# Hybrid encoder layer: eviction tiles and PSUM banks of the values' stage, early row scales, x first, a denser first attention

## The chip, the cores and the metric

One core of one Trainium2 chip runs the whole kernel. The metric is the device time of one execution in microseconds. The kernel before took 2954.69 us (median of 3 runs, 2953.99 to 2956.52).

## The reference, cut to what matters

One encoder layer is applied to two batches with the same weights: s (1024 tokens, two chunks of 512) and p (512 tokens, one chunk). The width is 2048, so there are 16 slices k of 128 features.

```
h  = rms_norm(x, norm_g) @ w_in      # split into qa ka va ga | qb kb vb gb
oa = window_gqa(qa, ka, va, sink, rel_bias)    # 16 heads, 4 key heads, +/-128 tokens
ob = diff_attention(qb, kb, vb, lam, ...)      # 8 heads, two softmax maps, RMSNorm per head
y  = rms_norm(x + concat(silu(ga) * oa, silu(gb) * ob) @ w_out, final_g)
```

Everything is float32. The kernel reaches that precision with three products of rounded numbers: each operand is split into a rounded part (hi, wh) and the remainder (lo, wl), and hi·wh + lo·wh + hi·wl is summed in PSUM.

## The kernel before, in words

**Stages.** The values' stage of batch s comes first (`in_v_all`, L357). It runs over five groups g of 256 value columns. For each group (`in_v`, L327) eight parts of the weights are used, two slices k each, and each part is 48 matmuls of 256 columns: 2 slices, 2 chunks, 4 token tiles, 3 products (L337, L339, L341). The sums of one group fill four PSUM banks, one bank for two token tiles of one chunk. At the end of a group eight evictions follow: ACT scales and rounds (L351), DVE makes the remainder (L352), both into one tile `ov`, and GpSimd's queue sends it to DRAM (L354). The pool `ev` has two tiles `ov`.

During group 0 the function `before` (L749) also loads x, splits it (L222, L223) and sums its squares. At the end of group 0 it makes the row scales by token (`rstd_cols`, L185, by products with a column of ones). During groups 1 to 4 it takes one step of `bias_rows` (L117) per part: constants, five small products of the bias tables (L130) with a copy to `o` (L132), and loads that spread the rows over 128 partitions. After group 4 `rstd_rows` (L194, called at L771) spreads the row scales over all partitions: four products per chunk with the identity, and a copy by DVE.

Then the feature stage of batch s follows (`in_fm`, L299; `project`, L281). It has 42 tiles of 128 features, each 16 slices times 6 matmuls of 512 columns. Its evictions (L310 to L324) use the tiles `o` and, under the name `sq`, `th`. Other places use the name `sq` too: the squares of `sum_squares` (L179) and those of `normalise` in the second attention (L617).

**Order of the work.** `drive` (L713) weaves a main generator (the projections) and a side one (attention). Each step of the projection reports its cost, and each step of attention is charged a fixed gap, so a smaller gap packs attention steps closer. While the features of s are projected, the first attention of s runs beside it with `GAP_AS` = 2.1. After it, in the same side generator, x of batch p is loaded, squared, summed and scaled (L778 to L788). In the second half the projections of p and all output projections run beside the second attention of s and both attentions of p; there the values' stage of p comes first, with one chunk and four evictions a group.

The source order is not the final order. The framework gives each instruction a place on its engine, by the order of the source and by when its inputs are ready. On each engine the instructions then run in order. A tile pool hands out one set of buffers for each name, and a new tile waits until the last user of its buffer is done. PSUM has eight banks. The pool `psv` of the values' stage has eight buffers under one name, `pp`. The next pool `psp1` takes over the four lower banks, and the attention's pools take the four upper ones.

**Queues.** SP issues nearly all loads, weights among them (`Weights.load`, L248, three tiles ahead). GpSimd's queue issues the stores.

**The lines that matter here.** L207 loads an x tile, L252 a weight tile, L260 and L262 split the weights. L328 takes the banks of a group, L348 the eviction tile:

```
ps = [[psp.tile([P, 2, 256], F32, name="pp") for _ in range(2)] for _ in chs]
...
o = ev.tile([P, 2, 256], F32, name="ov", bufs=2)
```

Of the kernel before, what the change touches and what calls it, by code (L numbers as in the profile page):

```python
# [9 lines left out]
F32 = mybir.dt.float32  # L10
# [20 lines left out]
LB = 2048  # L31
LA = 512
LATE = 4
GAP_AS = 2.1
GAP_BS = 1.05
GAP_AP = 1.7
GAP_BP = 1.3
# [7 lines left out]
def kernel(  # L45
# [71 lines left out]
    def bias_rows(psp, pool):  # L117
        constants()
        yield
        rb = const.tile([33, 24], F32, name="rb")  # L120
        nc.gpsimd.memset(rb[32:33], MASKED)
        dma(out=rb[0:32], in_=rel_bias)
        row_a = dram.tile([16, LA], F32, name="row_a")
        row_b = dram.tile([HB, LB], F32, name="row_b")
        for n in range(1 + LB // TC):
            oh = pool.tile([P, TC], F32, name="xr")
            dma(out=oh[0:33], in_=oh_a if n == 0 else oh_b[:, (n - 1) * TC:n * TC])
            m, heads = (16, rb[:, 0:16]) if n == 0 else (HB, rb[:, 16:24])
            ps = psp.tile([P, 512], F32, name="pp")
            T.matmul(ps[0:m, :], lhsT=heads, rhs=oh[0:33], start=True, stop=True)  # L130
            o = ev.tile([P, TC], F32, name="o", bufs=2)
            V.tensor_copy(o[0:m], ps[0:m, :])  # L132
            dma(out=row_a if n == 0 else row_b[:, (n - 1) * TC:n * TC], in_=o[0:m])
            yield
        for h in range(16):
            dma(out=rep_a[h], in_=row_a[h:h + 1, :].to_broadcast([P, LA]))
            yield
        for h in range(HB):
            dma(out=rep_b[h], in_=row_b[h:h + 1, :].to_broadcast([P, LB]))
            yield  # L140
# [41 lines left out]
        S.activation(out=dst, in_=src, func=AF.Sqrt, scale=1.0 / n, bias=eps)  # L182
        V.reciprocal(out=dst, in_=dst)

    def rstd_cols(acc, psp):  # L185

        ps = psp.tile([P, 512], F32, name="pp")
        for t in range(TC // P):
            T.matmul(ps[:, t:t + 1], lhsT=acc[:, t * P:(t + 1) * P], rhs=ones[:, 0:1], start=True, stop=True)
        rc = nrm.tile([P, TC // P], F32, name="rc", bufs=3)  # L190
        rsqrt_mean(rc, ps[:, 0:TC // P], DM)
        return rc

    def rstd_rows(rc, psp, pool=None, **kw):  # L194

        ps = psp.tile([P, 512], F32, name="pp")
        for t in range(TC // P):
            T.matmul(ps[:, t * P:(t + 1) * P], lhsT=rc[:, t:t + 1].to_broadcast([P, P]), rhs=ident, start=True, stop=True)
        if pool is None:
            return ps  # L200
        rb = pool.tile([P, TC], F32, name="rb", **kw)
        V.tensor_copy(rb, ps)
        return rb
# [37 lines left out]
    class Weights:  # L241


        def __init__(self, wp, order, loads, splits):
            self.wp, self.todo, self.loads, self.splits = wp, order, loads, splits
            self.raw, self.ready = [], []

        def load(self):  # L248
            while self.todo and len(self.raw) < self.loads:
                wr = self.wp.tile([P, 512], F32, name="wr", bufs=self.loads)  # L250
                src = self.todo.pop(0)
                dma(out=wr.rearrange("p (a c) -> p a c", a=src.shape[1]), in_=src)  # L252
                self.raw.append(wr)

        def split(self, n):
# [43 lines left out]
    def in_fm(b, chs, c, psp, wp):  # L299
        ps = yield from project(chs, psp, wp)  # L300
        gate = c >= C_GA
        f = 0.125 if c < C_KB or C_QA <= c < C_KA else 1.0
        for n, ch in enumerate(chs):
            sl = slice(n * TC, (n + 1) * TC)
            o = ev.tile([P, TC], F32, name="o", bufs=2)
            th = ev.tile([P, TC], F32, name="sq", bufs=2)
            hi = th.bitcast(F32R)
            h = ps[n]
            if not b.normed:
                V.scalar_tensor_tensor(out=o, in0=h, scalar=f, in1=b.rb[n], op0=ALU.mult, op1=ALU.mult)  # L310
                h = o
            if gate:
                S.activation(out=th, in_=h, func=AF.Tanh, scale=0.5)
                V.scalar_tensor_tensor(out=o, in0=th, scalar=1.0, in1=h, op0=ALU.add, op1=ALU.mult)
                pdma(out=b.fm[c][:, sl], in_=o)
                continue
            if b.normed:
                S.activation(out=hi, in_=h, func=AF.Copy, scale=f)
                V.scalar_tensor_tensor(out=o, in0=h, scalar=f, in1=th, op0=ALU.mult, op1=ALU.subtract)
            else:  # L320
                S.copy(out=hi, in_=o)
                V.tensor_tensor(out=o, in0=o, in1=th, op=ALU.subtract)
            pdma(out=b.fm[c][:, sl], in_=th)
            pdma(out=b.fml[c][:, sl], in_=o)  # L324
        done.add((b.nm, "fm", c))

    def in_v(b, chs, g, psp, wp, before=None):  # L327
        ps = [[psp.tile([P, 2, 256], F32, name="pp") for _ in range(2)] for _ in chs]  # L328
        for part in range(8):
            wh, wl = wp.next(2, before and (lambda: before(g, part)))  # L330
            for j in range(2):
                k = 2 * part + j
                for n, ch in enumerate(chs):
                    for t in range(4):
                        o = ps[n][t // 2][:, t % 2, :]
                        tok = slice(t * P, (t + 1) * P)
                        T.matmul(o, lhsT=ch.hi[k][:, tok], rhs=wh[:, j, :], start=(k == 0 and t % 2 == 0), stop=False,  # L337
                                 skip_group_check=True)
                        T.matmul(o, lhsT=ch.hi[k][:, tok], rhs=wl[:, j, :], start=False, stop=False,  # L339
                                 skip_group_check=True)  # L340
                        T.matmul(o, lhsT=ch.lo[k][:, tok], rhs=wh[:, j, :], start=False, stop=(k == KT - 1),  # L341
                                 skip_group_check=True)
                yield len(chs) * 12 * 0.109
        if before:
            before(g, 8)
        for n, ch in enumerate(chs):
            for t in range(4):
                o = ev.tile([P, 2, 256], F32, name="ov", bufs=2)  # L348
                f = 1.0 if b.normed else b.rc[n][:, t:t + 1]
                h = ps[n][t // 2][:, t % 2, :]  # L350
                S.activation(out=o[:, 0, :].bitcast(F32R), in_=h, func=AF.Copy, scale=f)  # L351
                V.scalar_tensor_tensor(out=o[:, 1, :], in0=h, scalar=f, in1=o[:, 0, :], op0=ALU.mult, op1=ALU.subtract)  # L352
                tok = slice(n * TC + t * P, n * TC + (t + 1) * P)
                pdma(out=b.v[g][tok], in_=o)  # L354
        done.add((b.nm, "v", g))

    def in_v_all(b, chs, psp, wp, before=None):  # L357
        for g in range(5):
            yield from in_v(b, chs, g, psp, wp, before)

    order_fm = []
    for pr in range(2):
# [372 lines left out]
    def run(g):  # L735
        for _ in g:
            pass
# [1 line left out]
    w_pool = lambda name, bufs: tc.tile_pool(name=name, bufs=bufs, reuse_waits="tile")  # L739

    with tc.tile_pool(name="act2", bufs=KT, side="right", reuse_waits="tile") as act2, w_pool("wp1", 2) as wp1:
        wp = Weights(wp1, tiles_v() + tiles_p(w_fm, order_fm), 3, 2)
        with tc.tile_pool(name="xraw1", bufs=9, side="right", reuse_waits="tile") as xraw, ps_pool("psv", 8, "left") as psp:
            chs = [new_chunk(), new_chunk()]
            accs = [xraw.tile([P, TC], F32, name="acc", bufs=2) for _ in chs]
            bias = bias_rows(psp, xraw)
            squares = []

            def before(g, part):  # L749
                if g > 0:  # L750
                    next(bias, None)
                    return
                late = squares[:] if part == 8 else squares[:-LATE]
                del squares[:len(late)]
                for n, sq in late:
                    V.tensor_tensor(out=accs[n], in0=accs[n], in1=sq, op=ALU.add)
                if part == 8:
                    bs.rc = [rstd_cols(acc, psp) for acc in accs]
                    return
                for k in (2 * part, 2 * part + 1):  # L760
                    for n in range(2):
                        xr = fetch(bs, n, k, xraw)
                        split_x(chs[n], xr, k, (act, act2)[n], ng[:, k:k + 1])
                        if k == 0:
                            sum_squares(accs[n], xr, True)
                        else:
                            squares.append((n, square(xr, xraw)))

            run(in_v_all(bs, chs, psp, wp, before))
            run(bias)  # L770
            bs.rb = [rstd_rows(rc, psp, nrm, bufs=2) for rc in bs.rc]  # L771

        with ps_pool("psp1", 4, "left") as psp, ExitStack() as held:
            raws = []
# [20 lines left out]
    with w_pool("wp2", 3) as wp2, ps_pool("psp2", 2, "left") as psp:  # L795
        wp = Weights(wp2, tiles_v() + tiles_p(w_fm, order_fm) + 3 * tiles_p(w_o, range(KT)), 3, 3)

        def main():
            yield from in_v_all(bp_, [ch_p], psp, wp)
            yield from in_fm_all(bp_, [ch_p], psp, wp)  # L800
            yield from need(("s", "a"), ("s", "b"))
            with tc.tile_pool(name="yp", bufs=1, reuse_waits="tile") as yp:
# [96 lines left out]
```

## Time and profile before

| | |
|---|---|
| median of 3 runs | 2954.69 us |
| the profiled execution | 2958.31 us |
| its span | 2956.5 us |
| mean granted clock of TensorE | 0.986 of 2.4 GHz |
| PE busy | 2884.3 us |
| DVE busy | 1601.6 us |
| ACT busy | 1142.4 us |

The span is the time from the first to the last instruction that the profile holds. The profiled execution's own time is 1.8 us longer than its span and 3.6 us longer than the median of the runs. Busy time of PE counts a matmul until its modelled end, so neighbouring matmuls overlap; the distance between two starts is the time that one takes from the next.

### The profile page before, as it was taken

Reading aid. Unit: us, or ns where it says so; the run is one execution under the profiler, and the core shown is the slowest. Engines: PE = TensorE matmul, PEld = TensorE weight load, DVE = VectorE, ACT = ScalarE, POOL = GpSimd, SP = SyncE. Lnnn points to the kernel's source line nnn. Section 1 sums busy time; section 2 is a strip of 40 time slices with the busy share of each in tenths; the row PEclk is TensorE's granted clock in tenths of the full one; section 3 lists DMA queues with packets and bytes.
Section 4 is the critical chain, followed back from the end, with each engine's and each line's share of the span. In section 5 each row is a group of like instructions: output and inputs, shape, how many; then the busy total and the mean of one; then the engine's idle time right before and its main releaser. Section 6 shows DMA issues by size and latency. Waiting matters only on the chain.

```text
span 2956.5 us, 42517 instructions
## 1 busy us (share of the span) xinstructions
PE 2884.3 (98%) x15370; PEld 2447.1 (83%) x15370; DVE 1601.6 (54%) x3328; ACT 1142.4 (39%) x2329; POOL 307.8 (10%) x554
## 2 busy tenths in 40 slices
PE   8998999999999999998999999999999999999997
PEld 8897888888888887888998888888887888788885
DVE  7122224555555555335666656666477766865633
ACT  6121113333333333124444444444355544543321
POOL 0010001111111111000010000000011100100101
PEclk9999999999999999999999999999999999999998
DMA  6732323342433433226454544443376557853633
GB/s 193 266 106 80 113 76 101 112 135 87 133 118 108 136 108 135 82 89 192 146 156 133 152 142 140 154 129 116 114 213 201 154 165 207 256 157 119 218 121 117
DMA packets 298686, 419.74 MB, mean 142 GB/s; under 512 B 49431, under 2 KB 164119, under 8 KB 297452
## 3 DMA queue, kind: packets, MB, share of 16 engines
q1 hardware_dynamic: 265452, 322.62, 36.4%
q0 software_dynamic: 33024, 94.41, 8.7%
q8 instruction: 121, 1.98, 0.3%
q14 instruction: 89, 0.73, 0.1%
HBM read 322.41 MB, written 107.05 MB: 145 GB/s over the span
## 4 chain that ended last, share of the span: by engine, by line
PE 75%; issue 18%; DMA 3%; DVE 1%; POOL 1%; ACT 1%; SPq 0%; POOLq 0%; DVEq 0%; ACTq 0%
PE pp L291 18%; PE pp L290 18%; PE pp L293 18%; PE s L566 4%; PE s L446 2%; PE tp L588 2%; PE tp L468 2%; PE pp L337 1%; PE pp L341 1%; PE pp L339 1%; PE o_ps L603 1%; PE o_ps L604 1%; PE o_ps L602 1%; PE o_ps L482 1%; PE o_ps L481 1%
## 5 line engine op out<-in xcount | busy, mean ns | idle before, releaser
L290 PE MATMUL pp<-hi,wh 128*128 128x512 f32 x2784 | 1124.9, 404 | 9.9 <-DVE ov L352 9.8
L291 PE MATMUL pp<-lo,wh 128*128 128x512 f32 x2784 | 1107.5, 398 | 0.8 <-DVE lo L236 0.8
L293 PE MATMUL pp<-hi,wl 128*128 128x512 f32 x2784 | 993.0, 396 | 0.6 <-DVE wl L262 0.6
L260 ACT CAST wh<-wr 128x512 fp32r<-128x512 f32 x608 | 375.9, 619 | 954.9 <-PE pp L291 672.8
L262 DVE TENSOR_TENSOR wl<-wr,wh 128x512 fp32r<-128x512 f32 x608 | 418.0, 688 | 558.8 <-ACT wh L260 525.4
L293 PEld LDWEIGHTS pp<-hi,wl 128*128 128x128 f32 x2784 | 525.7, 189 | 121.4 <-DVE wl L262 1.0
L290 PEld LDWEIGHTS pp<-hi,wh 128*128 128x128 f32 x2784 | 526.2, 189 | 106.6 <-DVE ov L352 10.0
L291 PEld LDWEIGHTS pp<-lo,wh 128*128 128x128 f32 x2784 | 526.9, 189 | 96.3 <-DVE lo L236 2.3
L337 PE MATMUL pp<-wh,hi 128*128 128x256 f32 x960 | 276.7, 289 | 19.8 <-ACT hi L222 8.6
L339 PE MATMUL pp<-wl,hi 128*128 128x256 f32 x960 | 272.9, 284 | 1.1 <-DVE wl L262 1.1
L341 PE MATMUL pp<-wh,lo 128*128 128x256 f32 x960 | 273.5, 285 | 0.0
L568 DVE CUSTOM_DVE_ANT_0 t<-s,strip 128x1024 f32<-128x1024 f32 (+1 forms) x192 | 199.5, 1042 | 84.1 <-PE s L566 83.8
L573 ACT ACTIVATE t<-t,nm 128x1024 f32<-128x1024 f32 (+1 forms) x192 | 193.6, 1008 | 125.7 <-DVE nm L568 124.1
L337 PEld LDWEIGHTS pp<-wh,hi 128*128 128x128 f32 x960 | 184.8, 193 | 27.1 <-ACT wh L260 9.4
L339 PEld LDWEIGHTS pp<-wl,hi 128*128 128x128 f32 x960 | 186.1, 194 | 2.6 <-DVE wl L262 1.8
L341 PEld LDWEIGHTS pp<-wh,lo 128*128 128x128 f32 x960 | 184.2, 192 | 0.1
L566 PE MATMUL s<-kk,qq 128*128 128x512 f32 x640 | 181.1, 396 | 1.9 <-DVE nm L568 1.8
L451 ACT ACTIVATE t<-t,nm 128x384 f32<-128x384 f32 (+1 forms) x192 | 110.0, 574 | 167.4 <-DVE nm L447 167.3
L591 DVE TENSOR_TENSOR pl<-tp,ph 128x512 fp32r<-128x512 f32 x160 | 110.1, 688 | 94.5 <-ACT ph L590 93.8
L471 DVE TENSOR_TENSOR pl<-tp,ph 128x512 fp32r<-128x512 f32 (+1 forms) x160 | 93.0, 582 | 107.5 <-ACT ph L470 106.9
L470 ACT CAST ph<-tp 128x512 fp32r<-128x512 f32 (+1 forms) x160 | 79.9, 500 | 181.5 <-PE tp L468 179.8
L447 DVE CUSTOM_DVE_ANT_0 t<-s,bias,nsink 128x384 f32<-128x384 f32 (+1 forms) x192 | 102.4, 570 | 73.2 <-PE s L446 73.2
(117 smaller groups left out, 2976.5 us busy)
## 6 DMA issues: line engine op xcount, KB each, us to landing
wr<-in_w_fm_dram SPq DMA_DIRECT2D x336, 256.0 KB, 3.2
wr<-in_w_o_dram SPq DMA_DIRECT2D x192, 256.0 KB, 3.5
wr<-in_w_v_dram SPq DMA_DIRECT2D x80, 256.0 KB, 3.5
xr<-in_xt_s_dram SPq DMA_DIRECT2D x64, 256.0 KB, 3.5
fm_s<-sq POOLq DMA_DIRECT2D x52, 256.0 KB, 3.6
fml_s<-o POOLq DMA_DIRECT2D x52, 256.0 KB, 3.8
out_dram<-y POOLq DMA_DIRECT2D x48, 256.0 KB, 3.9
v_s<-ov POOLq DMA_DIRECT2D x40, 256.0 KB, 2.5
```

What stands on the lines that cost most here:

```text
L260: S.copy(out=wh, in_=wr)
L262: V.tensor_tensor(out=wl, in0=wr, in1=raw(wh), op=ALU.subtract)
L290: T.matmul(ps[n], lhsT=wh[:, j, :], rhs=ch.hi[k], start=(k == 0), stop=False)
L291: T.matmul(ps[n], lhsT=wh[:, j, :], rhs=ch.lo[k], start=False, stop=False)
L293: T.matmul(ps[n], lhsT=wl[:, j, :], rhs=ch.hi[k], start=False, stop=(k == KT - 1))
L337: T.matmul(o, lhsT=ch.hi[k][:, tok], rhs=wh[:, j, :], start=(k == 0 and t % 2 == 0), stop=False, skip_group_check=True)
L339: T.matmul(o, lhsT=ch.hi[k][:, tok], rhs=wl[:, j, :], start=False, stop=False, skip_group_check=True)
L341: T.matmul(o, lhsT=ch.lo[k][:, tok], rhs=wh[:, j, :], start=False, stop=(k == KT - 1), skip_group_check=True)
L566: T.matmul(s[:, sl], lhsT=u.q[:, m, x, tok], rhs=u.head.kk[:, m, sl], start=(x == 0), stop=(x == 1))
L568: V.tensor_tensor_reduce(out=t, in0=s, in1=u.head.strip[:, x0:x0 + n], scale=-1.0, scalar=3.0e38, op0=ALU.add, op1=ALU.min, accum_out=u.nm ...
L573: S.activation(out=t, in_=t, func=AF.Exp, scale=-1.0, bias=u.nm[:, m:m + 1], accum_out=z1 if m else z0)
L591: V.tensor_tensor(out=pl[:, :, qi, :], in0=tp, in1=raw(ph)[:, :, qi, :], op=ALU.subtract)
```

## The change

- **Eviction tiles.** `in_v` gets a function `out(t)` for its tile. In the values' stage of s the tiles of t = 0 and 2 come from four buffers `ov` in the x pool, those of t = 1 from the two buffers `o`, those of t = 3 from the two buffers `th`. In the stage of p they alternate between `o` and `th`. The tile `th` of the feature stage gets this name of its own instead of `sq`, and the pool `ev` has no `ov` any more.
- **Banks.** The eight banks of the stage of s are two names of four, `p0` and `p1`. Even groups take `p0`, odd ones `p1`. The bias tables' and the row scales' products use `p0`, the column scales and the first identity products `p1`.
- **Row scales early.** `rstd_rows` is called in part 7 of group 1 instead of after group 4.
- **x first.** The first two x tiles are fetched before the first weights, and the first three weight tiles are issued from ACT's queue instead of SP's. Twenty products of the identity with itself stand ahead of everything on PE.
- **Buffers of the x pool.** x and squares have 8 buffers each instead of 9.
- **Denser first attention.** `GAP_AS` is 1.9 instead of 2.1.

```diff
-GAP_AS = 2.1
+GAP_AS = 1.9
@@ bias_rows
-            ps = psp.tile([P, 512], F32, name="pp")
+            ps = psp.tile([P, 512], F32, name="p0", bufs=4)
@@ rstd_cols, and rstd_rows in the same way
-        ps = psp.tile([P, 512], F32, name="pp")
+        ps = psp.tile([P, 512], F32, name=name, bufs=4 if name != "pp" else None)
@@ Weights
-                dma(out=wr.rearrange("p (a c) -> p a c", a=src.shape[1]), in_=src)
+                self.queue(out=wr.rearrange("p (a c) -> p a c", a=src.shape[1]), in_=src)
@@ in_fm
-            th = ev.tile([P, TC], F32, name="sq", bufs=2)
+            th = ev.tile([P, TC], F32, name="th", bufs=2)
@@ in_v
-        ps = [[psp.tile([P, 2, 256], F32, name="pp") for _ in range(2)] for _ in chs]
+        bufs = 4 if len(chs) > 1 else None
+        ps = [[psp.tile([P, 2, 256], F32, name=bank(g), bufs=bufs) for _ in range(2)] for _ in chs]
...
-                o = ev.tile([P, 2, 256], F32, name="ov", bufs=2)
+                o = out(t)
@@ the stage of s
-        wp = Weights(wp1, tiles_v() + tiles_p(w_fm, order_fm), 3, 2)
-        with tc.tile_pool(name="xraw1", bufs=9, ...) as xraw, ps_pool("psv", 8, "left") as psp:
+        wp = Weights(wp1, tiles_v() + tiles_p(w_fm, order_fm), 3, 2, S.dma_start)
+        with tc.tile_pool(name="xraw1", bufs=8, ...) as xraw, ps_pool("psv", 8, "left") as psp:
...
+            begin = psp.tile([P, 512], F32, name="p1", bufs=4)
+            for n in range(20):
+                T.matmul(begin[:, 0:P], lhsT=ident, rhs=ident, start=True, stop=True)
+            firsts = [fetch(bs, n, 0, xraw) for n in range(2)]
+            wp.load()
+            wp.queue = dma
@@ before
+                    if (g, part) == (1, 7):
+                        bs.rb = [rstd_rows(rc, psp, nrm, name="p0", bufs=2) for rc in bs.rc]
...
-                    bs.rc = [rstd_cols(acc, psp) for acc in accs]
+                    bs.rc = [rstd_cols(acc, psp, "p1") for acc in accs]
...
-                        xr = fetch(bs, n, k, xraw)
+                        xr = firsts[n] if k == 0 else fetch(bs, n, k, xraw)
@@ end of the stage
-            run(in_v_all(bs, chs, psp, wp, before))
+            pair = lambda pool, name, bufs: pool.tile([P, TC], F32, name=name, bufs=bufs).rearrange("p (x d) -> p x d", x=2)
+            out = lambda t: pair(xraw, "ov", 4) if t % 2 == 0 else pair(ev, ("o", "th")[t // 2], 2)
+            run(in_v_all(bs, chs, psp, wp, out, lambda g: f"p{g % 2}", before))
             run(bias)
-            bs.rb = [rstd_rows(rc, psp, nrm, bufs=2) for rc in bs.rc]
@@ main of the second half
-            yield from in_v_all(bp_, [ch_p], psp, wp)
+            out = lambda t: ev.tile([P, TC], F32, name=("o", "th")[t % 2], bufs=2).rearrange("p (x d) -> p x d", x=2)
+            yield from in_v_all(bp_, [ch_p], psp, wp, out)
```

## Rows read from the trace of the kernel before

**Rows 1.** The page: busy us, share of the span and instructions of each engine.

```profile
PE 2884.3 (98%) x15370; PEld 2447.1 (83%) x15370; DVE 1601.6 (54%) x3328; ACT 1142.4 (39%) x2329; POOL 307.8 (10%) x554
```

**Rows 2.** Waits of PE, whole span: line, releaser, us in total, times, longest.

```profile
PE pp L290 <- DVE ov L352: 9.8, 1, 9.8
...
PE pp L337 <- ACT hi L222: 8.6, 1, 8.6
...
PE s L566 <- DVE nm L568: 1.8, 5, 0.7
```

**Rows 3.** Windows: stretch, length, PE, PEld, DVE, ACT, POOL busy (x), granted clock, DMA share, GB/s.

```profile
150.00:200.00 50.00, 50.00 (x431) 50.00 (x431) 10.02 (x17) 9.28 (x17) 4.32 (x8) 1.00 0.27 91
...
700.00:800.00 100.00, 100.00 (x499) 83.34 (x498) 56.49 (x148) 37.72 (x94) 16.12 (x30) 1.00 0.38 114
...
126.00:128.00 2.00, 2.00 (x11) 2.00 (x10) 0.28 (x1) 0.47 (x1) 0.04 (x1) 0.50 1.03 289
```

**Rows 4.** Timeline, 112 to 142 us: start, duration, engine, line [idle before <- releaser].

```profile
123.11 0.47 ACT L351 ACTIVATE ov<-pp,rc 128x256 fp32r<-128x256 f32 x1 [6.55 <-DMA v_s<-ov]
...
124.14 0.38 PE L337 MATMUL pp<-wh,hi 128*128 128x256 f32 x1 [3.95 <-ACT wh L260]
...
125.46 0.41 PE L341 MATMUL pp<-wh,lo 128*128 128x256 f32 x1
...
128.86 0.28 PE L337 MATMUL pp<-wh,hi 128*128 128x256 f32 x1
```

**Rows 5.** Timeline, 0 to 14 us, and the row scales' products at 251 us.

```profile
1.11 0.29 POOL masks.py:199 TENSOR_SCALAR_AFFINE_SELECT ident<-ident 128x128 f32<-128x128 f32 x1
1.17 1.37 SPq L252 DMA_DIRECT2D wr<-in_w_v_dram  x3
...
7.83 0.72 ACT L222 ACTIVATE hi<-xr,ng 128x512 fp32r<-128x512 f32 x1 [0.73 <-DMA xr<-in_xt_s_dram]
...
8.98 0.41 PE L339 MATMUL pp<-wl,hi 128*128 128x256 f32 x1
...
12.76 0.31 PE L337 MATMUL pp<-wh,hi 128*128 128x256 f32 x1
...
251.07 1.95 PE L198 MATMUL pp<-ident,rc 128*128 128x128 f32 x16
```

**Rows 6.** Timeline, 1735 to 1776 us, ACT and PE.

```profile
1759.01 0.63 ACT L618 ACTIVATE sq<-osb 128x512 f32<-128x512 f32 x1 [5.79 <-DMA fm_p<-sq]
...
1762.01 3.57 PE L621 MATMUL tp<-ones,sq 128*128 128x1 f32 x16 [3.81 <-DVE pl L591]
...
1770.70 0.40 PE L290 MATMUL pp<-hi,wh 128*128 128x512 f32 x1
```

**Rows 7.** Waits of PE from 60 to 245 us.

```profile
PE pp L337 <- ACT wh L260: 4.5, 2, 3.9
PE pp L339 <- DVE wl L262: 0.7, 2, 0.3
```

**Rows 8.** Timeline: a pair of evictions on ACT, and PE at 262 us.

```profile
60.16 0.47 ACT L351 ACTIVATE ov<-pp,rc 128x256 fp32r<-128x256 f32 x1 [0.55 <-DVE ov L352]
...
262.81 0.79 PE L290 MATMUL pp<-hi,wh 128*128 128x512 f32 x1 [9.79 <-DVE ov L352]
...
268.52 0.53 PE L291 MATMUL pp<-lo,wh 128*128 128x512 f32 x1
```

**Rows 9.** Timeline, 1376 to 1402 us, ACT and PE.

```profile
1386.56 0.38 ACT L351 ACTIVATE ov<-pp 128x256 fp32r<-128x256 f32 x1 [4.18 <-DMA v_p<-ov]
...
1388.98 0.58 PE L337 MATMUL pp<-wh,hi 128*128 128x256 f32 x1 [3.41 <-DVE ov L352]
...
1395.12 0.33 PE L339 MATMUL pp<-wl,hi 128*128 128x256 f32 x1
```

**Rows 10.** Timeline, 1160 to 1182 us, PE.

```profile
1170.37 1.87 PE L189 MATMUL pp<-ones,acc 128*128 128x1 f32 x8 [4.70 <-DVE acc L179]
...
1180.06 0.46 PE L290 MATMUL pp<-hi,wh 128*128 128x512 f32 x1
```

More of the change, by code (lines that the diff above doesn't have):

```diff
@@ L183, in rsqrt_mean, with rstd_cols @@
         V.reciprocal(out=dst, in_=dst)
-    def rstd_cols(acc, psp):
-        ps = psp.tile([P, 512], F32, name="pp")
+    def rstd_cols(acc, psp, name="pp"):
+        ps = psp.tile([P, 512], F32, name=name, bufs=4 if name != "pp" else None)
         for t in range(TC // P):
@@ L192, in rstd_cols, with rstd_rows @@
         return rc
-    def rstd_rows(rc, psp, pool=None, **kw):
-        ps = psp.tile([P, 512], F32, name="pp")
+    def rstd_rows(rc, psp, pool=None, name="pp", **kw):
+        ps = psp.tile([P, 512], F32, name=name, bufs=4 if name != "pp" else None)
         for t in range(TC // P):
@@ L241, with __init__ @@
     class Weights:
-        def __init__(self, wp, order, loads, splits):
-            self.wp, self.todo, self.loads, self.splits = wp, order, loads, splits
+        def __init__(self, wp, order, loads, splits, queue=dma):
+            self.wp, self.todo, self.loads, self.splits, self.queue = wp, order, loads, splits, queue
             self.raw, self.ready = [], []
@@ L325, in in_fm, with in_v @@
         done.add((b.nm, "fm", c))
-    def in_v(b, chs, g, psp, wp, before=None):
-        ps = [[psp.tile([P, 2, 256], F32, name="pp") for _ in range(2)] for _ in chs]
+    def in_v(b, chs, g, psp, wp, out, bank, before=None):
+        bufs = 4 if len(chs) > 1 else None
+        ps = [[psp.tile([P, 2, 256], F32, name=bank(g), bufs=bufs) for _ in range(2)] for _ in chs]
         for part in range(8):
@@ L355, in in_v, with in_v_all @@
         done.add((b.nm, "v", g))
-    def in_v_all(b, chs, psp, wp, before=None):
+    def in_v_all(b, chs, psp, wp, out, bank=lambda g: "pp", before=None):
         for g in range(5):
-            yield from in_v(b, chs, g, psp, wp, before)
+            yield from in_v(b, chs, g, psp, wp, out, bank, before)
     order_fm = []
@@ L741 @@
     with tc.tile_pool(name="act2", bufs=KT, side="right", reuse_waits="tile") as act2, w_pool("wp1", 2) as wp1:
-        wp = Weights(wp1, tiles_v() + tiles_p(w_fm, order_fm), 3, 2)
-        with tc.tile_pool(name="xraw1", bufs=9, side="right", reuse_waits="tile") as xraw, ps_pool("psv", 8, "left") as psp:
+        wp = Weights(wp1, tiles_v() + tiles_p(w_fm, order_fm), 3, 2, S.dma_start)
+        with tc.tile_pool(name="xraw1", bufs=8, side="right", reuse_waits="tile") as xraw, ps_pool("psv", 8, "left") as psp:
             chs = [new_chunk(), new_chunk()]
```

## The prediction

> **What bounds the kernel now.** I read four views, in this order. The page's busy shares come first: PE is busy for 98% of the span, DVE and ACT for about half or less [rows 1]. So an edit pays only if it takes idle time, half-speed time or instructions from PE. The change removes no matmul and adds 20, so the gain can only lie in idle and half-speed time. Then the waits of PE, which sum over the whole run [rows 2]: the reader is to see that single waits make it up. One of 9.8 us that ends in L352, the eviction of the values' stage, and one of 8.6 us for the first split x are a quarter of the 72 us by which PE's busy time falls short of the span. Then the timeline around each of these waits, for what stood in front of the late instruction and for how long the matmuls after it are spaced at half speed. Last the windows of stretches without a wait, for what one matmul costs at full clock: 431 of 256 columns in 50 us, 0.116 us each [rows 3].
>
> A wait costs twice: the idle time, and then a stretch at the lower clock. After the 3.95 us wait in the first stage the 256-column records last 0.41 us from 125.46 on and 0.28 again at 128.86 [rows 4]; the granted clock there is 0.50, the 1.2 GHz level [rows 3]. Half of such a stretch is lost.
>
> **The start.** Before, PE begins after 8.6 us [rows 2], when the first split x is there, and its matmuls last 0.41 us until 12.76 [rows 5]. That stretch of 4.15 us yields what takes half of it later, so 2.07 us are lost. After, 20 products identity x identity fill one bank from the moment the identity is ready, 1.11 + 0.29 = 1.40 us [rows 5]. Eight products of the same kind are 16 records in 1.95 us, 0.122 us a record at full clock [rows 5], 0.244 at half. Twenty are 40 records: if the clock rises after 4.15 us again, 17 records pass in that time and 23 more take 2.8 us, 6.95 us in all, until about 8.5. Then the stage starts at full clock: 8.6 - 8.5 + 2.07 = **2.2 us gained**; I take 2.0. Bounds: if the slow stretch lasts 8.7 us, as after 1762.01 [rows 6], 36 records pass slowly and 4 fast, the products end at 10.7 and 2.1 - 2.07 = 0 is gained. If they don't lift the clock at all they end at 1.5 + 40 x 0.244 = 11.3, and the step costs 2.7 us. If 3.4 us are enough, as between 125.46 and 128.86 [rows 4], 2.6 us are gained.
>
> Of x moved first: three weight issues (1.37 us on SP [rows 5]) go to ACT's queue, and the two first x tiles move ahead of them on SP. ACT waits for data until 7.83 [rows 5], so 1.37 us lie beside a wait; without that cover they are the price. I cost the move at nothing more, since x is in at 7.83 even without it and the identity products end later.
>
> The Trainium skill (TensorE: Matmul & The Clock Gate, Part 4: PE-mode transpose) says that passes in transpose mode don't bring PE to its full clock. The added ones are ordinary matmuls, so I don't follow it here; by it the step would be +2.7 instead of -2.0. No row shows identity passes alone, so it stays a rival.
>
> **Eviction tiles in the first values' stage.** Before, 8 evictions of a group share 2 tiles and each pair waits until a DMA has landed. ACT is in order: its eviction waited 6.55 us for that DMA, the weight cast stood behind it, and PE waited 3.95 us for the cast [rows 4]; with a second such case 9 us later PE waited 4.5 us for the cast and 0.7 for DVE's difference after it, 5.2 in all [rows 7]. The slow stretch is 3.4 us, 1.7 lost. After, a group has 8 tiles (4 ov, 2 o, 2 th), none reused inside the group: **6.9 us gained**. Bound below: 0, if weights themselves land late in this busy stretch of DMA. Bias rows now take their o tile from the same two; a copy that waits for an eviction's DMA stalls DVE, with the weight difference behind it. The longest such wait seen is 6.55 us [rows 4]; a weight part is 48 matmuls, 5.6 us, and a split is one part ahead, so I cost it at 0 and keep 1 us as its end. One x and one square tile fewer: PE waited for x only once in the old stage, at its start [rows 2], so nothing; without cover one k step, 24 x 0.116 = 2.8 us.
>
> **Banks, and row scales made early.** The last group's matmuls end at 251; the eight products of the row scales follow (1.95 us [rows 5]), and the next stage's first matmul waits 9.79 us for the group's last eviction, because its bank is one of those [rows 8]. Half speed until about 268.7 is 5.9 us, 2.95 lost [rows 8]. After, the groups alternate between p0 and p1, four banks each. The name p1 is asked for first (the identity products), so it gets the pool's first four banks, which the next stage takes over; group 4 has p0. Its evictions then hold up nobody: **12.7 us gained**. The row scales' products move to the second group at the same 1.95 us on PE, and their two copies lie on a DVE that has 10 us of work in 50 [rows 3]. The new order of banks adds one wait: group 1 needs the banks of the column scales, whose ACT work ends about 1 us after group 1 starts; its first two banks are free, and 24 matmuls (2.8 us) cover it.
>
> **Eviction tiles in the prompt's values' stage.** Two tiles become four, for four evictions a group. Before, the third waits 4.18 us for a DMA, PE waits 3.41 us for its bank, and is slow from there to 1395.12, 6.1 us [rows 9]. Gain 3.41 + 3.05 = **6.4 us**. Below: 0, if DVE, busy with attention, evicts late anyway.
>
> **The new name th.** In the feature stage the tile th shared two buffers with the squares sq of attention B. At 1759.01 ACT's square ends a 5.79 us wait for a feature DMA out of such a buffer; PE waits 3.81 us behind it and is slow until 1770.70, 8.7 us [rows 6]. With th apart the square has its own buffer: 3.81 + 4.3 = **8.1 us gained**; below, 0.
>
> **Denser first attention (2.1 to 1.9).** Attention and projection share a PE that has no idle time between 700 and 800 [rows 3]; packing the same instructions closer moves work forward and leaves less attention to run later beside the same projection. DVE's 56 us in 100 would become about 60. I take 0. What it moves is the phase of the prompt's x loads, which follow this attention: there PE waits 4.70 us and is slow from 1170.37 to about 1180.2, 9.8 us, of which half is lost [rows 10]. This stall of 9.6 us may go, or grow by a weight part (5.6 us).
>
> **Sum.** -2.0 - 6.9 - 12.7 - 6.4 - 8.1 + 0 = -36.1 us. The profiled execution took 2958.31 us, 1.8 more than its span; 2958.31 - 36.1 = 2922.2. The median of the runs is 3.6 us lower, so **2918.6, rounded 2919 us**.
>
> **Rivals.**
> *Some waits only change hands* (0.18): in the prompt's stage the eviction is held by DVE's attention work, and the DMA of that square is followed by another late step. For: both stand in mixed stretches with DVE at about half. Against: the releaser is a DMA each time. Losing one or both of 6.4 and 8.1 gives 2925 to 2933.
> *The banks come the other way round* (0.07), so that the change doesn't do what it says: the feature stage sits on p0 and waits for the first two evictions of each bank. They come 1.03 us apart, 0.47 of work and 0.55 of wait [rows 8]: the second bank is free after 4.1 us, of which 0.46 is covered, and the slow stretch stays. 12.7 becomes 6.1 and the end is 2925.
> *The identity products don't lift the clock* (0.05), by that section of the skill as a mechanism of this kernel: 2919 + 4.7 = 2923.
> *Slower* (0.04): at 1.9 a unit's chain on DVE and ACT (bias, exponential, scale) no longer ends inside its steps, and PE waits for a score bank in the first attention. Only the second attention shows such a wait, 0.7 us at its longest [rows 2]. In each of its 64 units (4 key heads, 8 query blocks, 2 pairs) that is 45 us, 2964. It decides from 36.1/64 = 0.56 us a unit. Against it: at 2.1 PE waits for DVE nowhere at L446, the first attention's scores.
> *Hardly a change* (0.04): the gains of the first two stages are given back at the prompt's x loads and in new waits later.
> The forecast itself has 0.62, with 2909 to 2926 as its own range.
>
> **How the numbers follow.** Low end: the forecast with the prompt's x stall gone, 2909, and a faster start, 2908. High end: both mixed-stretch terms lost, 2933, or one lost and the prompt's stall a part longer, 2918.6 + 8.1 + 5.6 = 2932; I go to 2935 for small waits. About 0.2% (6 us) is what a measurement can tell from no change. Only the last two rivals end within that or above: faster 0.92, same 0.04, slower 0.04.
>
> **What would show it.** Right: PE's first 256-column records last 0.28 us and start near 8.5; no ACT eviction waits for a DMA of v; the first feature matmul follows the last values' matmul without idle time, near 244; no wait of ACT's square for a feature DMA; the prompt's second group starts without a wait. Wrong: a feature matmul that waits for L352, 0.41 us records after the identity products, a PE wait on L446 in the first attention, or a prompt x stall far from 10 us.

## The result, and the profile of the changed kernel

The changed kernel takes 2914.15 us (median of 4 runs, 2911.90 to 2918.75) against 2954.34 us of the kernel before beside it (4 runs, 2951.86 to 2956.52). The ratio is 0.9871, with a 95% interval of 0.9857 to 0.9885: 34 to 42 us faster. 2919 was predicted, in a range of 2908 to 2935. The profiled execution is the longest of the four, 2918.75 us with a span of 2917.0; the span before was 2956.5, so 39.5 us are to be placed.

For that the span is cut at instructions that both kernels have. The times are the starts of the first or last instruction of a line (column scales, feature matmuls, scores, matmuls of the values' stages); a stretch is the difference of two of them.

| stretch | before | after | difference | predicted |
|---|---|---|---|---|
| start to the first group's column scales | 56.3 | 59.1 | +2.8 | -2.0 |
| on to the first feature matmul | 206.5 | 188.8 | -17.7 | with the next |
| on to the first scores | 204.8 | 202.0 | -2.8 | -19.6 for both |
| on to the prompt's first values' matmul | 869.7 | 864.9 | -4.8 | 0 |
| that values' stage, first to last matmul | 189.7 | 181.0 | -8.7 | -6.4 |
| on to the last scores of the prompt's first attention | 860.0 | 851.7 | -8.3 | -8.1 |
| the rest of the span | 569.6 | 569.5 | -0.1 | 0 |
| span (rounded entries differ by 0.1) | 2956.5 | 2917.0 | -39.5 | -36.1 |

So the total was near. Two terms were off by the same 4.8 us in opposite directions (the start and the denser attention), and one, as the experiments show, was right in sum but given to the wrong edit. The last rows are less sure than the first: the rest of the span, which no edit of this study touches directly, takes 565.4 to 572.2 us in the traces of the thirteen kernels. First the page, the line that answers to [rows 1]: PE has 40 more records, those of the 20 identity products, and 14 us less busy time.

```profile
PE 2870.2 (98%) x15410; PEld 2432.3 (83%) x15410; DVE 1599.4 (55%) x3328; ACT 1141.7 (39%) x2329; POOL 309.4 (11%) x554
```

The waits of PE over the whole span of the changed kernel (line, releaser, us in total, times, longest), which answer to [rows 2]. The wait for L352's eviction is gone; the one for the first split x is 7.1 instead of 8.6 us. The scores of the second attention (L567) wait 2.3 us instead of 1.8. The row of the scores L447 for loads of queries (`fml_p`) belongs to the prompt's attention, at 2100 to 2122 us; the first attention of s has one wait at L447 worth naming, 1.07 us at 598.75, for which the profile shows no releaser.

```profile
PE p L338 <- ACT hi L222: 7.1, 1, 7.1
PE pp L189 <- DVE acc L179: 6.1, 4, 2.2
PE s L447 <- DMA qq<-fml_p: 2.5, 3, 1.0
PE pp L338 <- ACT wh L260: 2.4, 1, 2.4
PE s L567 <- DVE nm L569: 2.3, 5, 0.7
```

The start, timeline of PE (start us, duration, engine, line, count, [idle before <- releaser]), against [rows 5]. The reader is to see the order: ten matmuls of the stage at half speed (most of them 0.41 us), then the identity products, then the stage at full speed (0.28 us). The products were written first in the program, but the order in which the framework issues independent instructions put them eleventh.

```profile
7.12 0.58 PE L338 MATMUL p<-wh,hi 128*128 128x256 f32 x1 [7.12 <-ACT hi L222]
...
9.35 0.41 PE L338 MATMUL p<-wh,hi 128*128 128x256 f32 x1
9.57 6.03 PE L751 MATMUL p<-ident 128*128 128x128 f32 x40
15.35 0.37 PE L340 MATMUL p<-wl,hi 128*128 128x256 f32 x1
15.55 0.28 PE L342 MATMUL p<-wh,lo 128*128 128x256 f32 x1
```

The end of the first values' stage, timeline of PE and ACT, against [rows 8]: the feature matmul follows the last values' matmul without idle time, and after the first the evictions come 0.36 us apart, the sixth still ahead of the weight cast.

```profile
247.76 0.28 PE L342 MATMUL p<-wh,lo 128*128 128x256 f32 x1
247.88 0.40 PE L290 MATMUL pp<-hi,wh 128*128 128x512 f32 x1
...
247.80 0.48 ACT L352 ACTIVATE th<-p,rc 128x256 fp32r<-128x256 f32 x1
248.16 0.49 ACT L352 ACTIVATE ov<-p,rc 128x256 fp32r<-128x256 f32 x1
248.52 0.65 ACT L260 CAST wh<-wr 128x512 fp32r<-128x512 f32 x1
```

The prompt's column scales, timeline of PE, against [rows 10]: a wait of 0.99 us instead of 4.70. And a window of the stretch of [rows 3] in the first attention: DVE has 60.74 us of work in 100 instead of 56.49, and PE 0.37 us of idle time where it had none. The columns are those of [rows 3].

```profile
1098.62 1.05 PE L189 MATMUL pp<-ones,acc 128*128 128x1 f32 x8 [0.99 <-DVE acc L179]
```

```profile
700.00:800.00 100.00, 99.63 (x499) 82.29 (x498) 60.74 (x161) 40.12 (x101) 18.33 (x34) 1.00 0.45 130
```

The waits of [rows 4], [rows 6], [rows 7] and [rows 9] have no row in the changed kernel: between 60 and 245 us PE waits for nothing, no eviction of values waits for a DMA, and no square waits for a feature DMA (one square of the prompt's x waits 2.1 us for its x load).

### The profile page after: what moved, and what is told of

It reads as the page before. It is cut to its first block, busy times and chain, and to the rows that moved or that the text cites. A ratio compares the mean times of both kernels' runs of the same rounds, so it can differ in the third digit from the quotient of the medians.

```text
span 2917.0 us, 42569 instructions
## 1 busy us (share of the span) xinstructions
PE 2870.2 (98%) x15410; PEld 2432.3 (83%) x15410; DVE 1599.4 (55%) x3328; ACT 1141.7 (39%) x2329; POOL 309.4 (11%) x554
## 4 chain that ended last, share of the span: by engine, by line
PE 86%; issue 8%; DMA 2%; DVE 2%; ACT 1%; POOL 1%; SPq 0%; POOLq 0%; DVEq 0%; ACTq 0%
PE pp L291 19%; PE pp L290 19%; PE pp L293 19%; PE s L567 5%; PE p L338 3%; PE p L342 3%; PE p L340 3%; PE tp L589 2%; PE s L447 2%; PE tp L469 2%; PE pp L340 1%; PE pp L342 1%; PE pp L338 1%; PE o_ps L604 1%; PE o_ps L605 1%
## 5 line engine op out<-in xcount | busy, mean ns | idle before, releaser
L338 PE MATMUL p<-wh,hi 128*128 128x256 f32 x640 | 180.3, 282 | 7.1 <-ACT hi L222 7.1
L567 PE MATMUL s<-kk,qq 128*128 128x512 f32 x640 | 180.4, 395 | 2.4 <-DVE nm L569 2.3
L342 PE MATMUL p<-wh,lo 128*128 128x256 f32 x640 | 179.5, 280 | 0.0
L340 PE MATMUL p<-wl,hi 128*128 128x256 f32 x640 | 178.7, 279 | 0.0
L567 PEld LDWEIGHTS s<-kk,qq 128*128 128x128 f32 x640 | 117.3, 188 | 29.6 <-DVE nm L569 4.9
L591 ACT CAST ph<-tp 128x512 fp32r<-128x512 f32 x160 | 92.5, 578 | 96.4 <-PE tp L589 96.2
L338 PEld LDWEIGHTS p<-wh,hi 128*128 128x128 f32 x640 | 120.7, 189 | 11.4 <-ACT hi L222 7.1
```

The source lines that it names most:

```text
L567: T.matmul(s[:, sl], lhsT=u.q[:, m, x, tok], rhs=u.head.kk[:, m, sl], start=(x == 0), stop=(x == 1))
```

## The experiments

Each kernel is the changed one with the edit shown, but for the one under "The part alone", which is the kernel before with one part added. The medians are of 4 runs; the kernel before had 2954.61, 2953.93 and 2954.35 us beside the three batches. One run of a kernel differs from the next by 3 us and more, so a difference of 5 us is read from the stretches of the trace first; each trace is of one execution.

**The start: one product, products first, fourteen of them.**

```
-            for n in range(20):
-                T.matmul(begin[:, 0:P], lhsT=ident, rhs=ident, ...)
+            T.matmul(begin[:, 0:P], lhsT=ident, rhs=ident, ...)
```

> One of the 20 identity products is left, in the same place after ten matmuls of the stage. Theory (where they stand, the products only cost): in the changed kernel 40 records take 5.78 us, and PE is slow from 7.12 to about 11.4. With one product, about 8 of the stage's matmuls more run slowly (+0.9 us), and the column scales' products start 4.6 us earlier, at about 54.5 instead of 59.09; the whole is 4 to 5 us shorter than the changed kernel, about 2909.5. Rival 1 (the products buy the full clock): the slow stretch lasts 8.7 us or more, the column scales come at 56.6 or later. Rival 2 (the stage waits for x or weights anyway): they stay at 59, and the time is the same.

The column scales start at 54.2. PE's timeline: the single product, then slow records until 11.04, 3.7 us after the first matmul at 7.32.

```profile
9.77 0.63 PE L750 MATMUL p<-ident 128*128 128x128 f32 x2
...
10.83 0.40 PE L340 MATMUL p<-wl,hi 128*128 128x256 f32 x1
11.04 0.31 PE L342 MATMUL p<-wh,lo 128*128 128x256 f32 x1
11.19 0.28 PE L338 MATMUL p<-wh,hi 128*128 128x256 f32 x1
```

So the stage's own matmuls lift the clock as soon as the products do, and both rivals fall: where the products stand they cost 4.9 us. (The changed kernel's start is also that of five kernels below; their column scales come at 58.3 to 59.2.) The span is 4.7 us shorter than the profiled changed kernel's. The median, 2915.21 us (ratio 0.9871, 0.9856 to 0.9886), doesn't show it: the gain at the start is certain from the trace, the one in the whole is not.

```
+    ones = const.tile([P, P], F32, name="ones")
+    V.memset(ones, 1.0)
     ident = const.tile([P, P], F32, name="ident")
     make_identity(nc, ident)
-    ones = const.tile([P, P], F32, name="ones")
-    nc.gpsimd.memset(ones, 1.0)
...
-                T.matmul(begin[:, 0:P], lhsT=ident, rhs=ident, ...)
+                T.matmul(begin[:, 0:P], lhsT=ones, rhs=ones, ...)
```

> The 20 products take a tile of ones that VectorE sets as its first instruction, so they stand ahead of every other matmul on PE. Theory (the step failed by the place of the products alone): they start near 1.3 us, end between 7.7 and 8.5, the stage's first records last 0.28 us, and the column scales start at 53 to 53.5 instead of 59.09, 5.7 us earlier; the whole about 2908.5. Rival 1 (such products don't lift the clock): they end at 11.2, the next records last 0.41 us, the column scales come at 57 or later. Rival 2 (x and weights bound the stage once PE is early): idle time of PE appears inside the first group, and the column scales come no earlier than with one product (54.5).

2909.76 us (2908.75 to 2911.99; ratio 0.9852, 0.9836 to 0.9869), column scales at 52.8, 6.3 us earlier than in the changed kernel. PE's timeline:

```profile
1.05 7.16 PE L751 MATMUL p<-ones 128*128 128x128 f32 x40 [1.05 <-DVE ones L76]
7.96 0.37 PE L338 MATMUL p<-wh,hi 128*128 128x256 f32 x1
8.17 0.28 PE L340 MATMUL p<-wl,hi 128*128 128x256 f32 x1
```

This is what the prediction had described for the change, with 7.96 where it had 8.5. Against one product the twenty in front bring 1.4 us at the column scales. It is the fastest kernel of the study; its interval overlaps with that of the changed kernel, its slowest run is about the other's fastest.

With `range(14)` instead of `range(20)`:

> As the run with ones first, with 14 products instead of 20: 28 records. Theory: if the clock rises about 4.2 us after the first, they end near 6.9, just ahead of the first split x at 7.1, and the column scales start at 52 to 52.3, 7 us earlier than in the changed kernel; the whole about 2907. Rival (14 are too few, and the idle time behind them drops the clock): 0.41 us records after 7.1, column scales at 54 or later.

2914.53 us, column scales at 53.5. The records behind the products last 0.28 us, so the clock was up. The first comes at 7.49, 0.1 us after the last product, and by 15 us sixty records of the stage have started, as many as with twenty products. The 0.7 us are lost later: between 30 and 50 us 171 records start instead of 174. The number of products isn't shown to be the reason, because the kernel with the gap of 2.1, whose start is the changed kernel's own, also has 171 there, and the changed kernel 173; what sets this pace stays open. Both expectations missed, and this run shows neither a gain nor a loss from fewer products.

**Which banks: p0 asked for first.**

```
-            begin = psp.tile([P, 512], F32, name="p1", bufs=4)
+            begin = psp.tile([P, 512], F32, name="p0", bufs=4)
```

> The products write a bank of the name p0, so that name gets the pool's first four banks, which the feature stage takes over, and the last group sits on them. The products also come to stand first on PE. Theory: the column scales start at about 53.4, as with ones first, and after the last group PE waits 3 to 4 us for evictions and is slow for some 6 us, so the first feature matmul comes 3.6 us and the stage's next ones 6.6 us later than without; net 1 us above the changed kernel, about 2915. Rival (which of the two names lies on the first banks does not matter): no wait at the stage change, about 2908.5.

2918.20 us. Of the expectation only the rival's half on the banks holds. The identity products stand first and lift the clock, PE's timeline:

```profile
1.46 7.28 PE L751 MATMUL p<-ident 128*128 128x128 f32 x40 [1.46 <-POOL ident masks.py:199]
8.49 0.37 PE L338 MATMUL p<-wh,hi 128*128 128x256 f32 x1
8.70 0.28 PE L340 MATMUL p<-wl,hi 128*128 128x256 f32 x1
...
22.54 0.38 PE L338 MATMUL p<-wh,hi 128*128 128x256 f32 x1 [2.61 <-ACT wh L260]
```

This is the order that the prediction had in mind, and its 8.5 us for the start of the stage is met. But the order of the other engines moved too: ACT casts the weights behind a longer row of x work, PE waits 2.61 us for them, and the column scales come at 58.8. (The kernel with one name, below, also has this order, with a wait of 2.5 us and column scales at 58.3.) At the stage change, where by the order in which the names are asked for the feature stage now sits on the last group's banks (the trace doesn't name banks), no wait of note appears: from the column scales to the first feature matmul 189.1 us (changed kernel 188.8), on to the first scores 202.4 (202.0). The price of 6.6 us that the prediction gave to this order of banks is 0.7 us.

**Tiles against banks and row scales.** Two eviction tiles:

```
-            out = lambda t: pair(xraw, "ov", 4) if t % 2 == 0 else pair(ev, ("o", "th")[t // 2], 2)
+            out = lambda t: pair(xraw, "ov", 2)
```

> Two eviction tiles again in the first values' stage (only the name ov, two buffers); banks, row scales and all else as changed. Theory (the tiles hold the gain of both waits, inside the stage and at its end): PE waits about 5 us for weights inside the stage and is slow after it (6.9 us together), and at the end of the last group the weight cast that stands among ACT's evictions comes late, so that the first feature matmuls wait some us as well, although their banks are free; 7 to 15 us more than the changed kernel, 2921 to 2929. Rival (the prediction's own split: tiles 6.9, banks 12.7): the first feature matmuls start without a wait, and only the 6.9 us inside the stage come back, 2921.

2930.09 us (ratio 0.9926, 0.9903 to 0.9949). PE's waits up to 500 us, and ACT at the stage change:

```profile
PE p L338 <- ACT wh L260: 4.2, 1, 4.2
PE pp L290 <- ACT wh L260: 3.3, 1, 3.3
```

```profile
265.20 0.47 ACT L352 ACTIVATE ov<-p,rc 128x256 fp32r<-128x256 f32 x1 [5.09 <-DMA v_s<-ov]
...
270.27 1.13 ACT L260 CAST wh<-wr 128x512 fp32r<-128x512 f32 x2
```

The first feature matmul finds its bank free and starts at once, but the next weights' cast stands behind evictions that wait for DMAs, and PE stops one part later. From the column scales to the first scores it takes 404.3 us instead of 390.8: 13.5 more, as the theory had it, and not 6.9.

One name, row scales late (`"pp"` for `p0` and `p1`, the `rstd_rows` line behind `run(bias)`):

> One name for all eight banks of the stage and the row scales after the last group, as before; eight eviction tiles as changed. Theory (with eight tiles an eviction comes every 0.36 us, so the banks are free soon whichever they are): the row scales' 1.95 us come between, and the first feature matmul waits 1 to 2 us for the copy of the row scales, which stands behind the last evictions on DVE; with a slow stretch 2 to 5 us more than the changed kernel, 2916 to 2919. Rival (the prediction: the banks carry 12.7): PE waits near 10 us for the last eviction, 2927.

2916.90 us (ratio 0.9879, 0.9864 to 0.9894). PE and DVE at the stage change:

```profile
248.82 0.47 PE L290 MATMUL pp<-hi,wh 128*128 128x512 f32 x1 [1.57 <-DVE rb L202]
...
247.99 0.68 DVE L202 COPY rb<-pp 128x512 f32<-128x512 f32 x1
```

A wait of 1.57 us, as the theory had it; the rival's 10 us fall.

Row scales late, banks alternating:

> The row scales' products and copies after the last group again, in the banks p1; banks alternate and eight eviction tiles stay. Theory: their copies stand behind the last evictions on DVE, the feature stage's first two banks are theirs, PE waits 1 to 2 us for them and the whole is 1 to 4 us longer than changed, 2915 to 2918. Rival (nothing waits for them, since the copies end early enough): no wait of PE at the stage change, 2914. Second rival (they hold most of the 12.7): 2920 or more.

The same wait of 1.57 us for the same copy, and the same 190.5 us from the column scales to the first feature matmul as with one name. With eight tiles and late row scales, alternating the banks adds nothing that the trace shows; the early row scales are worth the 1.7 us. The median, 2919.26, is 5.1 us above the changed kernel's; 1.7 of these have a cause in this stage, the rest I can't place.

**The part alone**, on the kernel before. As in the changed kernel, x and squares have 8 buffers each; the prompt's two tiles get the name `o`:

```
-                o = ev.tile([P, 2, 256], F32, name="ov", bufs=2)
+                o = out(t)
...
+            pair = lambda pool, name, bufs: pool.tile(...).rearrange("p (x d) -> p x d", x=2)
+            out = lambda t: pair(xraw, "ov", 4) if t % 2 == 0 else pair(ev, ("o", "sq")[t // 2], 2)
```

> The kernel before with eight eviction tiles in its first values' stage and nothing else: one name for the banks, row scales after the stage, no products at the start, gap 2.1, two tiles in the prompt's stage, sq shared. Theory (the tiles carry most of what the prediction gave to banks and row scales): no wait inside the stage, and the first feature matmul waits 1.6 us for the copy of the row scales instead of 9.8 us; it starts near 248, the stretch after it is not slow for long, and the whole is 16 to 19 us below the kernel before, 2935 to 2938. Rival (the prediction's split): only 6.9 us go, the wait of 9.8 us stays, 2947.

2939.43 us (ratio 0.9937, 0.9917 to 0.9957), 14.9 us below the kernel before by the medians, and 20.3 by the spans of the profiled executions. From the column scales to the first scores it takes 391.9 us instead of 411.3: 19.4 us by the tiles alone (with the smaller x pool, which wasn't tested by itself). The first feature matmul waits 0.9 us and not the 1.6 expected, for a remainder of the evictions and not for the copy of the row scales. PE's waits up to 500 us hold one row for this stage change:

```profile
PE pp L290 <- DVE sq L352: 0.9, 1, 0.9
```

The stretch from the column scales to the first scores in the four corners, in us. The gap of the attention doesn't enter it: with 2.1 the changed kernel has 390.8 too.

| | one name, late row scales | alternating, early |
|---|---|---|
| two tiles | 411.3 (before) | 404.3 |
| eight tiles | 391.9 (before with tiles), 392.6 (changed with one name) | 390.8 (changed) |

**The denser attention.** `GAP_AS = 2.1`:

> The first attention's gap at 2.1 again, all else as changed. Theory (the gap moved the prompt's x loads to where the weights' loads leave room): PE's wait for the accumulated squares before the prompt's column scales comes back, 4 to 5 us, with its slow stretch; the first matmul of the prompt's values' stage starts 4.5 to 9.6 us later than in the changed kernel (1314.8), the whole 2918.5 to 2924. Rival 1 (the other changes moved the loads): no difference, 2914. Rival 2 (the denser attention costs waits that the wider gap spares): first matmul of the prompt's values earlier than 1314.8.

2920.03 us. From the first scores to the prompt's first values' matmul 869.1 us instead of 864.9. PE's waits from 500 to 1320 us:

```profile
PE pp L189 <- DVE acc L179: 4.9, 1, 4.9
```

The stall of [rows 10] is back. The stretch grows by 4.2 us and the prompt's values start 3.9 us later, a little under the 4.5 expected: without the stall the denser attention has small waits that the wider gap doesn't have. In this stretch PE is idle for 8.1 us before, 8.2 at 2.1 and 5.2 in the changed kernel.

**The name th.**

```
-            th = ev.tile([P, TC], F32, name="th", bufs=2)
+            th = ev.tile([P, TC], F32, name="sq", bufs=2)
```

> The feature stage's second eviction tile shares the name sq with the squares of the second attention again; all else as changed. Theory (the prediction's term of 8.1): ACT's square waits near 5 us for a feature DMA, PE waits 3 to 4 us at the products of the squares and is slow behind it; from the prompt's first feature tiles to the end of the second attention some 8 us are lost, the whole 2920 to 2923. Rival (the other changes moved the square away from the DMA): no such wait, 2914 to 2915.

2928.68 us (ratio 0.9908, 0.9892 to 0.9925): more than expected, since it shows in two places. ACT and PE in the timeline:

```profile
1097.71 0.63 ACT L172 ACTIVATE sq<-xr 128x512 f32<-128x512 f32 x1 [4.76 <-issue]
1104.11 1.05 PE L189 MATMUL pp<-ones,acc 128*128 128x1 f32 x8 [3.58 <-DVE acc L179]
...
1732.26 0.63 ACT L619 ACTIVATE sq<-osb 128x512 f32<-128x512 f32 x1 [5.73 <-DMA fm_p<-sq]
```

The last line is the stall of [rows 6]; the stretch from the end of the prompt's values to its last scores takes 859.2 us instead of 851.7, 7.5 more. The first two lines are another user of the name: the squares of the prompt's x are made under `sq` as well (L172, in the helper that L179 calls), and one of them stands 4.76 us behind the feature evictions at 1091 and 1092 that hold both buffers. The profile names no releaser there, but the first of the two outgoing DMAs, issued at 1092.20, landed 5.4 us later at 1097.64, just ahead of this square. The stretch up to the prompt's values takes 869.0 us, 4.1 more than in the changed kernel.

**The prompt's tiles.** `name="o"` for `name=("o", "th")[t % 2]`; the feature stage uses the name too:

> The prompt's values' stage evicts through one name with two buffers again; all else as changed. Theory (the prediction's term of 6.4): ACT waits near 4 us for a DMA of the values, PE 3.4 us for its bank, a slow stretch follows; the stretch from the stage's first matmul to its last grows from 181.0 us to 187.4 or more, the whole 2920 to 2923. Rival (DVE's attention work sets the eviction): 181 to 183, the whole 2914 to 2916.

2925.88 us (ratio 0.9895, 0.9877 to 0.9912). The stage takes 192.2 us instead of 181.0, more than expected: three waits for evictions, 6.3 us together, where the expectation had one of 3.4. PE's waits, and ACT's, from 1300 to 1510 us:

```profile
PE pp L338 <- DVE o L353: 6.3, 3, 3.7
```

```profile
ACT o L352 <- DMA v_p<-o: 10.8, 5, 4.4
```

## Why the prediction was right or wrong

**The total** was right in the main for a reason that stands: the change takes waits behind DMAs out of ACT's in-order queue, PE gets its weights and banks in time, and long waits removed give back a slow stretch too. That it came out so near is also luck: the start cost 2.8 us where 2.0 were to be gained, the denser attention gained 4.8 where 0 was put down, and these two errors cancel. Two of the signs that the prediction named for being wrong did appear, a wait at the scores of the first attention (1.07 us, once) and a stall of the prompt's x far from 10 us (0.99).

**The start failed.** The step "20 products identity x identity fill one bank from the moment the identity is ready" supposed that they come first on PE because they are written first. They came after ten real matmuls, at 9.57, and cost 4.9 us there (against one product). The x-first part, costed at nothing, gained: the first stage matmul waits 7.1 instead of 8.6 us. This wait varies, 6.3 to 7.3 us in seven traces with x first that start with a stage matmul, 8.6 and 7.9 in the two without, so 1.3 us is a better estimate than 1.5. Once the products do come first, the step's working on PE holds, the stage at full clock from 7.96 (ones) or 8.49 (identity). The gain holds in part: with ones the column scales are 3.5 us ahead of the kernel before (52.8 against 56.3), but one product already has 2.1 of that, so the products bring 1.4 where the step had 2.0. With the identity first, as the step supposed, the gain is lost again to the 2.61 us wait for a weight cast (58.8). The rival that the products don't lift the clock falls: ahead of the stage they do, of ones and of the identity (records of 0.28 us right behind them). The passage of the Trainium skill (TensorE: Matmul & The Clock Gate, Part 4: PE-mode transpose) that was weighed there is about transposes; no run here has those alone.

**Tiles and banks: the sum right (20.5 measured, 19.6 predicted), the split wrong.** The prediction gave 6.9 to the tiles and 12.7 to banks and row scales. The tiles alone bring 19.4; banks and row scales add 1.1 to 1.8 to them. The step that failed is the rate of evictions: "They come 1.03 us apart, 0.47 of work and 0.55 of wait", and a wait of 9.79 us for the last of them, were taken over from a stage with two tiles. That rate was itself made by the two tiles (ACT waiting for DVE and for DMAs). With eight it is 0.36 us, and in the changed kernel the last remainder ends at 250.7, 2.6 us after the last values' matmul. The edits are not additive: with two tiles the banks and the early row scales bring 7.0, with eight 1 to 2. The bank order, a rival at 6.6, is worth 0.7 at most for the same reason. The Trainium skill (Perfetto Trace Analysis, Optimizing Tensor Performance, Matmuls) says that independent groups of matmuls should rotate through PSUM banks so that evictions overlap the next group. The first group after a stage change is such a case, and in these runs rotation, together with the early row scales, was worth 7.0 us only while the evictions were held up by something else.

**The prompt's values' stage** was right in mechanism and mis-sized: 8.7 us for 6.4. The term took the one wait of 3.41 us; the stage had three waits for evictions, 4.3 us together, of which only the long one has a slow stretch (granted clock 0.50 from 1388.38 to 1395.20). PE's idle time in the stage falls from 6.4 to 2.8 us, and half of that slow stretch is 3.4. The 1.6 us that are left aren't due to the tiles: behind the stage's first wait, for a weight cast, the clock was at 0.50 for 6.8 us before and for 3.4 in the changed kernel. With the same tiles the stage takes 179.4 us in the kernel with two tiles `ov`, where the clock doesn't fall there at all, and 181.8 in the one with late row scales.

**The name th**: 8.3 measured in its stretch, 8.1 predicted, and 7.5 given back when it is undone. What the step didn't see is that the prompt's squares use the same name.

**The denser attention** was costed at 0, with the stall of the prompt's x, 9.6 us by the prediction's count, left open in both directions. Nearly the whole stall goes, but only 4.8 us are gained there. So the denser packing itself costs some 4 us in this stretch, an estimate: PE has 1.8 us of small waits beside the stall, which the kernel before doesn't have, and its busy time falls by 1.9 us (861.6 to 859.7) where half of the slow stretch would be 4.9. For the gain two edits are needed together: with the gap of 2.1 the stall is back, and with the shared name at 1.9 it is back too. Why the x loads come out better at 1.9 is read from the trace only in part: the column scales come at 1098.6 instead of 1152.6 at 2.1; which neighbouring load gives way wasn't tested. The rival "slower" falls in its size: PE waits at the scores of the first attention once, 1.07 us, and not in each unit.

## What to carry to other kernels

When two edits both work on one queue (here evictions that wait for their DMA, in order with the weight casts), price them together: a rate read beside the bottleneck is the bottleneck's rate, and it goes when the bottleneck goes. Look for all users of a tile's name before a price is put on renaming it. Compare a forecast with the result term by term, stretch by stretch: here two errors of 4.8 us cancelled and the sum didn't show them. And where a framework orders independent instructions, an instruction written first isn't first: read its place in the engine's order, and make its operand the first thing that is ready.

## What the runs showed of the hardware that was not expected

The lower clock doesn't always begin with the first matmul after a wait. At the prompt's first values' matmul in the changed kernel (timeline of PE) PE waits 2.38 and 0.69 us, runs a record of 0.28 us, is at 0.42 from 1316.51 and back at 0.28 at 1319.88: 3.4 us at half speed, and the loss comes behind the work that was late. After longer waits in the kernel before it had fallen by then: the feature matmul behind the wait of 9.79 us lasts 0.79 us [rows 8], where 0.40 is usual. So the slow stretch is looked for in the records behind a wait, not only in the first.

```profile
1314.82 0.50 PE L338 MATMUL pp<-wh,hi 128*128 128x256 f32 x2 [2.38 <-ACT wh L260]
1316.01 0.39 PE L340 MATMUL pp<-wl,hi 128*128 128x256 f32 x1 [0.69 <-DVE wl L262]
1316.22 0.28 PE L342 MATMUL pp<-wh,lo 128*128 128x256 f32 x1
...
1316.51 0.42 PE L340 MATMUL pp<-wl,hi 128*128 128x256 f32 x1
...
1319.88 0.28 PE L338 MATMUL pp<-wh,hi 128*128 128x256 f32 x1
```
